# Weights packed by the host in the order of the chip's loads: a hybrid mixer block on one Trainium2 core

## The chip, the cores and the metric

The kernel runs on one core of one Trainium2 chip. The metric is device microseconds of one execution (lower is better). The kernel before takes 2065.49 us, the median of three runs (2064.67 to 2066.31). The host's work ahead of the launch, its packing of arrays included, is not in the time.

## The reference, cut to what matters

One block over 256 latent tokens and 256 context tokens of width D = 2048, all in float32. Six adaLN vectors come from a 2048 x 12288 matrix; the modulated tokens go through one wide projection, four groups of mixers (GLA, gated delta rule, a short convolution, RWKV-7), an output projection, and a SwiGLU of width 5632.

```python
def _modulation(cond, w, bias):
    m = jax.nn.silu(cond) @ w + bias
    return [a[:, None, :] for a in jnp.split(m, 6, axis=-1)]

m_x = _modulation(c, ada_w[l], ada_b[l])
m_c = _modulation(c_ctx[None, :], ada_w[l], ada_b[l])
o_c, ctx_states = _mix(_modnorm(h_c, norm1_g[l], m_c[0], m_c[1]), h_c.shape[1], zero, lp)
o_x, _ = _mix(_modnorm(h_x, norm1_g[l], m_x[0], m_x[1]), GRID_W, ctx_states, lp)   # n @ w_in ... y @ w_out
h_x = h_x + m_x[2] * o_x
h_x = h_x + m_x[5] * _swiglu(_modnorm(h_x, norm2_g[l], m_x[3], m_x[4]), ffn_w_gu[l], ffn_w_down[l])
return _rmsnorm(h_x, final_g)
```

Every weight is read from HBM: `ada_w` once (96 MB), `w_in` twice (context and latents), `w_out`, `w_gu` and `w_down` once.

## The kernel before, in words

P = 128 is a tile's width, KT = 16 the number of feature tiles, T = 256 the tokens of a sequence. Products are exact to float32: each weight tile `wraw` is split by ScalarE into an upper half `wh` (L156) and by VectorE into the rest `wl` (L161), and TensorE (PE) adds three products of halves. All loads of weights are issued by SyncE (SP) on one queue, in program order. The program has four stages.

**Start.** The context tokens (`xin`, two loads of 1 MB) are normed and turned. Then a loop over 16 feature tiles kt: `first_vectors(kt)` loads two 1 MB pieces of `ada_w` into `ad` (three buffers, L391), multiplies them with the two conditions (`ada`, 32 PE instructions), and makes the modulated tokens `nh`, `nl`; `early_weights(kt)` loads one row tile of 11 column tiles of `w_in` into `wr` (three buffers; seven loads, L415 and L419, 704 KB) and splits it; PE then adds 33 products into `acc`. PE takes the `ada` products of tile kt + 1 ahead of the `acc` products of tile kt.

**Mixers.** `proj` loads a column tile of `w_in` in four pieces of 256 KB into `wraw` (six buffers, L571) and adds its products into `big`; between them stand `ada_pieces`, steps of the later adaLN vectors: a 256 KB load (L255) and products into `ob`. The recurrences of the mixers (`la`, `lb`, `ea`, `eb`, `iv...`) run beside them. `spill` parks a projected tile in DRAM (`xr...<-xs`, L596), `fetch` loads it again (L602). The order of the pieces is written by hand in `ORDER`, with offsets in instructions; the order of single instructions is then settled by the tile scheduler from its own estimates of how long each step takes.

**Output projection** (`wout`, L1376, 256 KB loads) and **SwiGLU** (`w_gu` L1445 and `w_down` L1482, 512 KB loads into four wide buffers).

In each of these loads a partition of the chip reads rows of the reference's matrices, so that what lies together in HBM is 128 columns (512 bytes) in `ada_w`, `w_in` and `w_gu`, and 512 columns (2 KB) in `w_out`, `w_down` and two pieces of each `wr`.

Of the kernel before, what the change touches and what calls it, by code (L numbers as in the profile page):

```python
# [16 lines left out]
P = 128  # L17
D = 2048
# [26 lines left out]
LEVS = (16, 32, 64)  # L45

# [86 lines left out]

@with_exitstack
def block_kernel(ctx: ExitStack, tc: tile.TileContext, x, cx, ada_w, ada_b, w_in, w_out, w_gu, w_down,
                 final_g, consts, params, small, out):
# [105 lines left out]
    gate_dram = mk(dram, [2, D], "gated")  # L242

    def ada_pieces(ci, bank_of, tmp):
        """adaLN columns of one of the later vectors, in steps to be taken between other work"""
        st = {}

        def piece(j, kt):
# [3 lines left out]
            with tc.high_priority():  # L252
                raw = wraw()
                rv = raw.rearrange("p (g c) -> p g c", g=4)
                nc.sync.dma_start(rv, ada_w[kt * P:(kt + 1) * P, ci * D:(ci + 1) * D]  # L255
                                  .rearrange("p (g c) -> p g c", g=4)[:, :, j * P:(j + 1) * P])
# [37 lines left out]
    def open_bank(flat):  # L294
        """zeros in a PSUM bank, left open for sums in any order"""
# [21 lines left out]
    # block-diagonal tiles: off-diagonal blocks stay zero  # L317
# [21 lines left out]
    RUNS = [(n, NR) for n in ("r_k", "r_v")] + [(n, ND) for n in ("d_k", "d_v")]  # L339
    EARLY = [(n, i) for n, k in RUNS for i in range(k)]  # L340
# [4 lines left out]
    with ExitStack() as st:  # L345
# [37 lines left out]
        NE = len(EARLY) + 1  # L383
# [3 lines left out]
        def first_vectors(kt):  # L387
            """modulation of feature tile kt, and the modulated context tokens"""
            ad = mk(s0, [P, KT, 2, P], "ad", 3)
            for i in range(2):  # L390
                nc.sync.dma_start(ad[:, :, i, :], ada_w[:, i * D + kt * P:i * D + (kt + 1) * P]  # L391
                                  .rearrange("(k p) c -> p k c", p=P))
# [18 lines left out]
        def early_weights(kt):  # L411
            raw = mk(s0, [P, NE * P], "wr0", 3)
            rows = slice(kt * P, (kt + 1) * P)
            for (c0, w, c) in SMALLS:
                nc.sync.dma_start(raw[:, c:c + w], w_in[rows, c0:c0 + w])  # L415
            o = P
            for n, k in RUNS:
                if k:
                    nc.sync.dma_start(raw[:, o:o + k * P], w_in[rows, OFF[n]:OFF[n] + k * P])  # L419
                o += k * P  # L420
# [42 lines left out]
    def col_products(ps, wh, wl, a, first, last):  # L463
        """ps[:, 0] + ps[:, 1] += w @ a, w and a in exact halves"""
# [4 lines left out]
    def row_products(acc, aH, aL, wh, wl, first, last, j):  # L469
        """acc[j] += a @ w for one half of the tokens; a is stored transposed, both in exact halves"""  # L470
# [5 lines left out]
    # ================= mixers =================  # L476
    Y = mk(dram, [16, P, T], "Yd")
    with mix:
# [4 lines left out]
        def runsum(o, i, d, z):  # L483
            """running sums, forward or backward, starting anew where z is zero"""
# [12 lines left out]
        # recurrent states at the end of the context, parked  # L497
# [64 lines left out]
        def proj(nHL, segs):  # L562
            """w_in columns of segs, transposed: [columns, tokens] in PSUM"""
            H, L = nHL
            ps = PB([P, T], "big")
            for hf in range(4):
                with tc.high_priority():
                    raw = wraw()
                    rv = raw.rearrange("p (k c) -> p k c", k=4)
                    for (c0, w, o) in segs:  # L570
                        nc.sync.dma_start(rv[:, :, o:o + w],  # L571
                                          w_in[hf * 512:(hf + 1) * 512, c0:c0 + w].rearrange("(k p) c -> p k c", p=P))
# [12 lines left out]
        def pcol(nHL, name, i):  # L585
            return proj(nHL, [(OFF[name] + i * P, P, 0)])
# [4 lines left out]
        def spill(nHL, name, i, s=1):  # L591
            """project columns and park them"""
# [14 lines left out]
        def sigmoid(o):  # L607
            """o = sigmoid(o), o not under -87"""
# [4 lines left out]
        def silu_to(o, z, tag):  # L613
            """o = z * sigmoid(z)"""
# [14 lines left out]
            # diagonal blocks, one row per partition  # L629
# [5 lines left out]
            # rows r and 15 - r of a block hold 15 entries together; side by side, the second one backwards  # L635
# [8 lines left out]
            # all entries of a block on every partition of that block  # L644
# [72 lines left out]
        def smalls(sm):  # L717
            """gate inputs of low rank, and what hangs on them alone"""
            cur[0] = "b"
            # rows 0..15: inputs of the GLA gate; 32..39: running sums of the GDN log decay;  # L720
            # 64..127: shifted RWKV inputs
# [6 lines left out]
            for d in range(2):  # L728
# [7 lines left out]
                # tanh(z) = 2 sigmoid(2 z) - 1  # L736
# [6 lines left out]
            # Gated DeltaNet: log decay, its running sums, beta  # L743
# [4 lines left out]
            # softplus(z) = -logsig(-z)  # L748
# [22 lines left out]
            # sums over whole chunks, on every partition  # L771
# [5 lines left out]
            # rows 0..3 (forward) use the running sum, rows 4..7 (backward) the reversed one  # L777
# [19 lines left out]
        def rw_gates(p, d, sm):  # L797
            """sums of sigmoid(.) inside each chunk of 64 (the log decay over -RW_S), and a"""
# [21 lines left out]
        def halves(dst, src, eng):  # L820
            """src [P, 4, 64] -> the diagonal blocks of dst [P, 4, 2, 64]"""
# [18 lines left out]
        def rwkv(p, s, raw, sm):  # L840
# [6 lines left out]
            for d in range(2):  # L847
# [52 lines left out]
                # values, token-major  # L900
# [5 lines left out]
                # L and M  # L906
# [9 lines left out]
                # decayed keys, token-major  # L916
# [5 lines left out]
                # [nB | nA^T]  # L922
# [9 lines left out]
                # [K~ | A_rk^T], token-major  # L932
# [31 lines left out]
                for n, c in enumerate(order):  # L964
                    # [outputs | state]
# [37 lines left out]
        def conv(o, z, taps, s):  # L1003
            """three-tap convolution along rows of 256 (context) or 64 tokens"""
# [9 lines left out]
        def gdn(h, s, raw, sm):  # L1014
# [40 lines left out]
            # decays between tokens; index d * 2 + c  # L1055
# [95 lines left out]
        def gla(p, s, raw, sm):  # L1151
# [28 lines left out]
            for d in range(2):  # L1180
# [52 lines left out]
                for n, c in enumerate((0, 1, 2, 3) if d == 0 else (3, 2, 1, 0)):  # L1233
                    # [outputs | state]
# [85 lines left out]
        for tok in ORDER:  # L1320
            st, _, ofs = tok.partition(":")
            with tc.high_priority(offset=int(ofs)) if ofs else ExitStack():
# [8 lines left out]
                elif low == "xx":  # L1331
                    if c == 0:
                        nHL = load_nT()
                        smx = t1("rgate")
                        acopy(smx, proj(nHL, SMALLS))
# [36 lines left out]
        def wout(b, kts, acc):  # L1372
            for kt in kts:
                with tc.high_priority():
                    raw = wraw()
                    nc.sync.dma_start(raw, w_out[kt * P:(kt + 1) * P, b * 512:(b + 1) * 512])  # L1376
# [52 lines left out]
    # ================= SwiGLU =================  # L1429
# [5 lines left out]
    for f in range(FT):  # L1435
        # sums of the products with the tokens' upper parts, and with their lower ones
        pg = [mk(ps2, [P, 2, T], "acc", 8) for _ in range(2)]
        for k0, nk, bufs in ((0, 8, wide), (8, 4, narrow), (12, 4, narrow)) if f == 0 else ((0, 8, wide), (8, 8, wide)):
            w = []
            wp[:] = bufs  # L1440
            for u in range(2):
                c0 = u * FFN + f * P
                with tc.high_priority():
                    raw = wraw()
                    nc.sync.dma_start(raw.rearrange("p (k c) -> p k c", k=nk),  # L1445
                                      w_gu[k0 * P:(k0 + nk) * P, c0:c0 + P].rearrange("(k p) c -> p k c", p=P))
                    w.append(split(raw, V))
            # the first tile takes the tokens as they get ready
# [16 lines left out]
    # the table of the last norm's functions, ahead of it  # L1465
# [7 lines left out]
    for b in range(4):  # L1473
# [3 lines left out]
        for k2 in range(FT // 2):  # L1477
            # the last weights of all are kept for the halves of the tokens in turn
            tail = b == 3 and k2 >= FT // 2 - 4
            with tc.high_priority():  # L1480
                raw = wraw()
                nc.sync.dma_start(raw.rearrange("p (k c) -> p k c", k=2),  # L1482
                                  w_down[k2 * 256:(k2 + 1) * 256, sl].rearrange("(k p) c -> p k c", p=P))
# [27 lines left out]
def prepare(inputs):  # L1511
    """host side: arrays as the launch takes them"""
# [24 lines left out]
```

## Time and profile before

| what | value |
|---|---|
| time, median of 3 runs | 2065.49 us |
| span of the profiled execution | 2059.4 us |
| what lies around the span (median less span) | 6.1 us |
| start, up to 200 us | DMA engines busy 0.94 to 1.01 up to 184 us |
| mixers, output projection, 200 to 1320 us | PE busy 1070.1 of 1120 us |
| SwiGLU, 1333 to 2050 us | PE busy 716.6 of 717 us |

The span is from the first to the last instruction of one profiled execution; it is the profile's only time of it, so times below are from the span's start, and the 6.1 us around it are carried over. PE busy counts a matmul from its start to a modelled end, so that it overlaps with its neighbours. PEclk is the clock that was granted to TensorE, as a share of 2.4 GHz: 0.5 is 1.2 GHz. The DMA share is the mean busy share of the core's 16 DMA engines, and GB/s what they moved.

### The profile page before, as it was taken

What the parts mean: (1) busy time and instruction counts of PE and PEld (TensorE: products, weight loads), DVE (VectorE), ACT (ScalarE), POOL (GpSimd) and SP (SyncE); (2) the same over time, 40 slices, a digit from 0 to 9 for tenths busy, and PEclk for the clock granted to TensorE, in tenths of its full rate; (3) what the DMA queues carried; (4) which work ended last, traced back from release to release, by engine and by line L of the source; (5) the groups of instructions that cost most, each with busy time, mean ns of one, the idle gap of its engine ahead of it and who ended that gap; (6) DMA issues with size and microseconds to landing.
All of it is one profiled execution on the core that took longest, in us unless ns stands there. A gap on an engine that the chain in (4) does not pass through costs nothing.

```text
span 2059.4 us, 37523 instructions
## 1 busy us (share of the span) xinstructions
PE 1933.2 (94%) x13864; PEld 1640.5 (80%) x13864; DVE 1341.9 (65%) x3488; ACT 988.3 (48%) x2013; POOL 163.3 (8%) x210
## 2 busy tenths in 40 slices
PE   4777999979999999999999999899999999999998
PEld 2556787758887887888989978788888888888886
DVE  3333875788778957889897776655555555545554
ACT  2112644564456435555654565555555555544444
POOL 0000100000101000101010000200000000000000
PEclk9899999989999999999999999999999999999999
DMA  9997858834847748534333655466666666665554
GB/s 271 277 275 222 240 162 236 228 103 125 227 139 199 204 140 246 136 82 111 102 105 107 166 186 193 135 187 188 187 185 185 188 188 186 185 234 195 193 195 154
DMA packets 609272, 374.31 MB, mean 182 GB/s; under 512 B 31776, under 2 KB 570784, under 8 KB 608192
## 3 DMA queue, kind: packets, MB, share of 16 engines
q1 hardware_dynamic: 604176, 366.59, 61.3%
q10 hardware_dynamic: 4320, 3.15, 0.5%
q8 instruction: 109, 1.79, 0.4%
q0 software_dynamic: 592, 2.18, 0.3%
q14 instruction: 75, 0.61, 0.1%
HBM read 359.89 MB, written 11.94 MB: 181 GB/s over the span
## 4 chain that ended last, share of the span: by engine, by line
PE 73%; DMA 11%; DVE 8%; issue 3%; ACT 2%; POOL 1%; SPq 0%; ACTq 0%; DVEq 0%; POOLq 0%
PE acc L173 36%; PE big L173 14%; PE la L173 8%; DMA ad<-in_ada_w 6%; PE ea L173 4%; PE lb L173 4%; PE ob L173 3%; PE eb L173 3%; DVE wl L161 2%; DMA wraw<-in_w_in 2%; DMA wraw<-in_ada_w 1%; ACT wh L156 1%; DMA wr<-in_w_in 1%; DVE ivaXc L161 1%; DVE ivaw L161 1%
## 5 line engine op out<-in xcount | busy, mean ns | idle before, releaser
L161 DVE TENSOR_TENSOR wl<-wraw,wh 128x512 fp32r<-128x512 f32 x856 | 568.3, 690 | 417.8 <-ACT wh L156 410.0
L156 ACT ACTIVATE wh<-wraw 128x512 fp32r<-128x512 f32 x856 | 509.9, 625 | 544.6 <-PE acc L173 186.2
L173 PE MATMUL acc<-n,wh 128*128 128x512 f32 x1408 | 493.4, 399 | 3.0 <-ACT wh L156 3.0
L173 PE MATMUL acc<-n,wl 128*128 128x256 f32 x1408 | 382.7, 282 | 0.3 <-DVE wl L161 0.3
L173 PE MATMUL big<-nh,wh 128*128 128x256 f32 x1056 | 319.5, 303 | 0.9 <-ACT xs L156 0.9
L173 PE MATMUL big<-nl,wh 128*128 128x256 f32 x1056 | 308.2, 292 | 0.0
L173 PE MATMUL big<-nh,wl 128*128 128x256 f32 x1056 | 306.7, 291 | 1.2 <-DVE wl L161 1.2
L173 PEld LDWEIGHTS acc<-n,wh 128*128 128x128 f32 x1408 | 259.9, 189 | 59.9 <-ACT wh L156 3.3
L173 PEld LDWEIGHTS acc<-n,wl 128*128 128x128 f32 x1408 | 266.9, 190 | 9.3 <-DVE wl L161 0.8
L173 PEld LDWEIGHTS big<-nh,wh 128*128 128x128 f32 x1056 | 199.7, 189 | 29.6 <-issue 23.5
L173 PEld LDWEIGHTS big<-nh,wl 128*128 128x128 f32 x1056 | 199.9, 190 | 8.1 <-issue 5.2
L173 PEld LDWEIGHTS big<-nl,wh 128*128 128x128 f32 x1056 | 199.9, 189 | 7.3 <-issue 6.7
L173 PE MATMUL acc<-wl,hH 128*128 128x512 f32 x352 | 137.1, 389 | 0.0
L173 PE MATMUL acc<-wh,hH 128*128 128x512 f32 x352 | 137.0, 389 | 0.0
L173 PE MATMUL acc<-wh,hL 128*128 128x512 f32 x352 | 137.0, 389 | 0.0
L173 PE MATMUL ob<-wraw,sc 128*32 128x128 f32 x2048 | 110.4, 284 | 10.7 <-DMA wraw<-in_ada_w 7.0
L173 PEld LDWEIGHTS ob<-wraw,sc 128*32 128x32 f32 x2048 | 52.1, 109 | 45.4 <-DMA wraw<-in_ada_w 12.1
L173 PE MATMUL ada<-ad,sc 128*32 128x256 f32 x512 | 46.0, 510 | 37.6 <-DMA ad<-in_ada_w 35.5
L161 POOL TENSOR_TENSOR hL<-sg,hH 128x256 fp32r<-128x256 f32 x44 | 44.5, 1012 | 453.4 <-ACT hH L156 453.4
L173 PEld LDWEIGHTS acc<-wl,hH 128*128 128x128 f32 x352 | 66.1, 188 | 14.2 <-DVE wl L161 0.2
L173 PEld LDWEIGHTS acc<-wh,hH 128*128 128x128 f32 x352 | 66.1, 188 | 13.7
L173 PEld LDWEIGHTS acc<-wh,hL 128*128 128x128 f32 x352 | 66.1, 188 | 13.6
(473 smaller groups left out, 3130.6 us busy)
## 6 DMA issues: line engine op xcount, KB each, us to landing
wraw<-in_w_gu SPq DMA_DIRECT2D x174, 512.0 KB, 4.0
wraw<-in_w_in SPq DMA_DIRECT2D x260, 256.0 KB, 3.0
wraw<-in_ada_w SPq DMA_DIRECT2D x256, 256.0 KB, 3.7
wraw<-in_w_down SPq DMA_DIRECT2D x88, 512.0 KB, 4.3
ad<-in_ada_w SPq DMA_DIRECT2D x32, 1024.0 KB, 8.4
wraw<-in_w_out SPq DMA_DIRECT2D x64, 256.0 KB, 3.2
wr<-in_w_in SPq DMA_DIRECT2D x32, 256.0 KB, 4.0
xin<-in_cx SPq DMA_DIRECT2D x2, 1024.0 KB
```

Of the source, the lines that this page charges most:

```text
L156: A.activation(o, i, AF.Copy)
L161: (e or V).tensor_tensor(out=o, in0=a, in1=b, op=op)
L173: return TE.matmul(o, l, r, start=start, stop=stop)
```

## The change

The host lays each weight matrix out anew, so that one load reads for each partition one run: 2 KB for a piece of `w_in`, `w_out` and the later adaLN vectors, 4 KB for `w_gu` and `w_down`, 5632 bytes for a row tile of the early weights (a copy of their columns of its own, `w_early`), 8 KB for half of an `ad`. The same bytes land at the same places on chip. Three things change beside the runs: the seven loads of a `wr` are one, the three or more loads of a `SMALLS` piece in `proj` are one (12 loads become 4), and the two loads of an `ad` split it by the summed features, not by shift and scale. Comment lines are gone too, which moves line numbers.

```diff
@@ ada_pieces: piece
-                nc.sync.dma_start(rv, ada_w[kt * P:(kt + 1) * P, ci * D:(ci + 1) * D]
-                                  .rearrange("p (g c) -> p g c", g=4)[:, :, j * P:(j + 1) * P])
+                r0 = (((ci - 2) * 4 + j) * KT + kt) * P
+                nc.sync.dma_start(raw, ada_later[r0:r0 + P, :])
@@ first_vectors
             ad = mk(s0, [P, KT, 2, P], "ad", 3)
+            av = ada_first[kt * P:(kt + 1) * P, :].rearrange("p (k a c) -> p k a c", k=KT, a=2)
             for i in range(2):
-                nc.sync.dma_start(ad[:, :, i, :], ada_w[:, i * D + kt * P:i * D + (kt + 1) * P]
-                                  .rearrange("(k p) c -> p k c", p=P))
+                ks = slice(i * KT // 2, (i + 1) * KT // 2)
+                nc.sync.dma_start(ad[:, ks], av[:, ks])
@@ early_weights
             raw = mk(s0, [P, NE * P], "wr0", 3)
-            rows = slice(kt * P, (kt + 1) * P)
-            for (c0, w, c) in SMALLS:
-                nc.sync.dma_start(raw[:, c:c + w], w_in[rows, c0:c0 + w])
-            o = P
-            for n, k in RUNS:
-                if k:
-                    nc.sync.dma_start(raw[:, o:o + k * P], w_in[rows, OFF[n]:OFF[n] + k * P])
-                o += k * P
+            nc.sync.dma_start(raw, w_early[kt * P:(kt + 1) * P, :])
@@ proj
-                    rv = raw.rearrange("p (k c) -> p k c", k=4)
-                    for (c0, w, o) in segs:
-                        nc.sync.dma_start(rv[:, :, o:o + w],
-                                          w_in[hf * 512:(hf + 1) * 512, c0:c0 + w].rearrange("(k p) c -> p k c", p=P))
+                    nc.sync.dma_start(raw, w_in[r0:r0 + P, hf * 512:(hf + 1) * 512])
@@ wout
-                    nc.sync.dma_start(raw, w_out[kt * P:(kt + 1) * P, b * 512:(b + 1) * 512])
+                    nc.sync.dma_start(raw, w_out[(b * KT + kt) * P:(b * KT + kt + 1) * P, :])
@@ SwiGLU
-                    nc.sync.dma_start(raw.rearrange("p (k c) -> p k c", k=nk),
-                                      w_gu[k0 * P:(k0 + nk) * P, c0:c0 + P].rearrange("(k p) c -> p k c", p=P))
+                    nc.sync.dma_start(raw, w_gu[r0:r0 + P, k0 * P:(k0 + nk) * P])
...
-                nc.sync.dma_start(raw.rearrange("p (k c) -> p k c", k=2),
-                                  w_down[k2 * 256:(k2 + 1) * 256, sl].rearrange("(k p) c -> p k c", p=P))
+                r0 = (b * (FT // 2) + k2) * P
+                nc.sync.dma_start(raw, w_down[r0:r0 + P, :])
```

The scheduler settles the order anew with the changed loads. On SP, in the start's loop, this stood before for one feature tile (destination, source, shape, how often):

```order
L415 DMA wr_77_241<-in_w_in 128x32 x2
L415 DMA wr_77_241<-in_w_in 128x64
L419 DMA wr_77_241<-in_w_in 128x512 x2
L419 DMA wr_77_241<-in_w_in 128x128 x2
L391 DMA ad_253<-in_ada_w 128x16x128 x2
```

And this stands there now, for the first three feature tiles:

```order
L446 DMA wr_77_241<-in_w_early 128x1408
L425 DMA ad_247<-in_ada_first 128x2048 x2
L446 DMA wr_85_278<-in_w_early 128x1408
L425 DMA ad_284<-in_ada_first 128x2048 x2
L446 DMA wr_93_348<-in_w_early 128x1408
L425 DMA ad_354<-in_ada_first 128x2048 x2
```

The order of `wr` and `ad` is the same; nine issues of a feature tile have become three.

On PE, where the start's loop begins, the turns of the tokens (`pt<-ident,xin`, four to a pair of feature tiles) stood before ahead of the first `ada` products like this:

```order
L374 MATMUL pt_195<-ident_64,xin_161 128x128
L374 MATMUL pt_195<-ident_64,xin_169 128x128
...
L374 MATMUL pt_201<-ident_64,xin_161 128x128
L374 MATMUL pt_201<-ident_64,xin_169 128x128
...
L173 MATMUL ada_256<-ad_253,sc_82 32x256 x5
L374 MATMUL pt_207<-ident_64,xin_161 128x128
```

Now the first of them stands behind the first of eight turns:

```order
L407 MATMUL pt_177<-ident_64,xin_161 128x128
L407 MATMUL pt_177<-ident_64,xin_169 128x128
...
L208 MATMUL ada_250<-ad_247,sc_82 32x256
L407 MATMUL pt_183<-ident_64,xin_161 128x128
L407 MATMUL pt_183<-ident_64,xin_169 128x128
```

The first `ada` product has moved from behind the fifth turn to behind the first; eight products of the second `ada` now stand between the last turns too.

On SP, in the middle of the mixers, where the latents' first RWKV keys are parked (`xr_r_k<-xs`), this stood before; the weights of that tile's projection end with `wraw_8376`, 7 loads of `w_in` ahead of the store:

```order
L571 DMA wraw_8566<-in_w_in 128x4x128
L255 DMA wraw_8572<-in_ada_w 128x4x128
L255 DMA wraw_8578<-in_ada_w 128x4x128
L571 DMA wraw_8596<-in_w_in 128x4x128
L596 DMA xr_r_k_1853_8407<-xs_8284 128x256
L602 DMA gd_rk_7773<-xr_d_z_1503_6871 128x256
L255 DMA wraw_8602<-in_ada_w 128x4x128
```

And this stands there now, where that projection's weights end with `wraw_8272`, 5 loads of `w_in` ahead of the store:

```order
L596 DMA wraw_8397<-in_w_in 128x512
L291 DMA wraw_8403<-in_ada_later 128x512
L291 DMA wraw_8409<-in_ada_later 128x512
L596 DMA wraw_8432<-in_w_in 128x512
L291 DMA wraw_8438<-in_ada_later 128x512
L620 DMA xr_r_k_1853_8303<-xs_8180 128x256
L291 DMA wraw_8444<-in_ada_later 128x512
```

The store has moved forward by two loads of `w_in` and the pieces of `ada` between them; many parks and fetches of the mixers have moved by a few loads like this, forward or back.

## Rows read from the trace of the kernel before

**Rows 1.** The page: busy time of each engine, and the DMA engines' slices.
```profile
span 2059.4 us, 37523 instructions
PE 1933.2 (94%) x13864; PEld 1640.5 (80%) x13864; DVE 1341.9 (65%) x3488; ACT 988.3 (48%) x2013; POOL 163.3 (8%) x210
DMA  9997858834847748534333655466666666665554
```

**Rows 2.** Windows by stage: busy us (x instructions) by engine, PEclk, DMA share, GB/s.
```profile
39.00:184.00 145.00, 108.51 (x1003) 86.53 (x1007) 49.34 (x88) 25.62 (x30) 0.00 (x0) 0.89 1.01 276
184.00:200.00 16.00, 10.56 (x95) 8.42 (x96) 5.60 (x17) 3.40 (x9) 2.92 (x9) 0.89 0.28 103
200.00:1320.00 1120.00, 1070.08 (x8878) 914.82 (x8877) 873.97 (x2677) 582.98 (x1238) 101.83 (x141) 0.99 0.58 163
1333.00:2050.00 717.00, 716.60 (x3758) 612.30 (x3756) 391.90 (x660) 356.77 (x703) 53.67 (x50) 1.00 0.62 189
```

**Rows 3.** The chain that ended last, 39 to 184 us: shares, and two pieces.
```profile
by line: DMA ad<-in_ada_w 81.4%; DMA wr<-in_w_in 11.9%; PE ada L173 5.4%; SPq L391 2.4%; SPq L419 1.9%; issue 1.5%; SPq L415 1.0%; PE acc L173 0.5%; DVE n L167 0.3%; PE pt L173 0.2%; DVE modB L165 0.2%; DVE modA L167 0.1%
...
60.26 9.92 DMA ad<-in_ada_w
...
173.81 10.00 DMA ad<-in_ada_w
```

**Rows 4.** Timeline of the start: second and last `ada`, and what precedes the loop.
```profile
18.62 1.91 ACT L286 ACTIVATE junk<-xin 128x2048 f32<-128x2048 f32 x1 [3.43 <-DMA xin<-in_cx]
...
24.24 1.12 PE L374 MATMUL pt<-ident,xin 128*128 128x128 f32 x4 [0.78 <-DVE xnT L381]
...
26.14 1.12 PE L374 MATMUL pt<-ident,xin 128*128 128x128 f32 x4 [0.78 <-DVE xnT L381]
...
36.44 2.64 ACT L156 ACTIVATE wh<-wr 128x1408 fp32r<-128x1408 f32 x2 [15.26 <-PE pt L374]
38.35 1.63 DVE L161 TENSOR_TENSOR wl<-wr,wh 128x1408 fp32r<-128x1408 f32 x1
39.17 3.18 PE L173 MATMUL ada<-ad,sc 128*32 128x256 f32 x32 [1.26 <-DMA ad<-in_ada_w]
...
183.95 1.93 PE L173 MATMUL ada<-ad,sc 128*32 128x256 f32 x32
```

**Rows 5.** Timeline of one feature tile's work on PE, and the next wait.
```profile
100.88 1.93 PE L173 MATMUL ada<-ad,sc 128*32 128x256 f32 x32 [1.66 <-DMA ad<-in_ada_w]
...
107.10 0.28 PE L173 MATMUL acc<-nh,wl 128*128 128x256 f32 x1
...
111.72 3.42 PE L173 MATMUL ada<-ad,sc 128*32 128x256 f32 x32 [4.34 <-DMA ad<-in_ada_w]
```

**Rows 6.** Windows in which the DMA engines moved one kind of run.
```profile
15.00:16.00 1.00, 0.00 (x0) 0.00 (x0) 0.78 (x1) 0.19 (x1) 0.00 (x0) 1.00 0.99 408
183.00:186.00 3.00, 2.74 (x39) 1.72 (x38) 0.06 (x1) 0.00 (x0) 0.00 (x0) 1.00 0.97 395
1450.00:1550.00 100.00, 100.00 (x568) 86.92 (x567) 55.49 (x98) 51.44 (x105) 9.16 (x9) 1.00 0.64 186
1900.00:2000.00 100.00, 100.00 (x443) 82.81 (x442) 54.97 (x82) 45.13 (x82) 6.42 (x4) 1.00 0.58 195
```

**Rows 7.** DMA issues: out<-in, count, KB of each, median us to landing.
```profile
ad<-in_ada_w SPq DMA_DIRECT2D x32, 1024.0 KB, 8.4
...
consts<-in_consts SPq DMA_DIRECT2D x1, 898.0 KB
...
sw<-in_small SPq DMA_DIRECT2D x1, 768.0 KB
```

**Rows 8.** Line 571, loads of `w_in`: issues, who waited, us to landing.
```profile
L571 SPq DMA_DIRECT2D wraw<-in_w_in x272: 367/368/1222, 0.7 to 1182.1; - x136
...
  ACT wh L156: 83.9, 57
...
DMA to landing us min/median/max: 2.6/3.1/5.2
```

**Rows 9.** Line 1376, loads of `w_out` (2 KB runs): issues, us to landing.
```profile
L1376 SPq DMA_DIRECT2D wraw<-in_w_out x64: 327/328/664, 1183.5 to 1285.1; - x64
...
DMA to landing us min/median/max: 2.9/3.2/7.3
```

**Rows 10.** The chain through the mixers, 218 to 1320 us: shares, first and last weight load.
```profile
by line: PE big L173 25.8%; PE la L173 14.3%; PE ea L173 8.3%; PE lb L173 7.6%; PE ob L173 5.1%; PE eb L173 4.8%; DVE wl L161 4.4%; issue 3.9%; DMA wraw<-in_w_in 3.0%; DMA wraw<-in_ada_w 2.6%; ACT wh L156 2.3%; DVE ivaXc L161 1.1%; DVE ivaw
...
291.33 3.58 DMA wraw<-in_w_in
...
1139.24 2.88 DMA wraw<-in_w_in
```

**Rows 11.** A window of the mixers in which PE idled most.
```profile
400.00:450.00 50.00, 37.89 (x265) 27.68 (x263) 41.42 (x126) 26.20 (x62) 1.69 (x3) 0.86 0.47 131
```

More of the change, by code (lines that the diff above doesn't have):

```diff
@@ L45 @@
 LEVS = (16, 32, 64)
+TILES = ([("small", 0)] + [(n, i) for n, k in (
+    ("r_k", 4), ("r_v", 4), ("r_r", 4), ("d_k", 4), ("d_v", 4), ("d_q", 4), ("d_z", 4), ("g_k", 2), ("g_q", 2),
+    ("g_v", 4), ("g_r", 4), ("r_g", 1), ("c_c", 4), ("c_h", 4), ("c_b", 4)) for i in range(k)])
+TIDX = {t: i for i, t in enumerate(TILES)}
+RUNS = [(n, NR) for n in ("r_k", "r_v")] + [(n, ND) for n in ("d_k", "d_v")]
+EARLY = [(n, i) for n, k in RUNS for i in range(k)]
+NE = len(EARLY) + 1
 def _const_array():
@@ L131, in _pack_small, with _pack_w_in, cols, _pack_ada @@
     return out
+def _pack_w_in(w):
+    def cols(n, i):
+        if n == "small":
+            return np.concatenate([w[:, c0:c0 + k] for c0, k, _ in SMALLS], 1)
+        return w[:, OFF[n] + i * P:OFF[n] + (i + 1) * P]
+    tiles = np.stack([cols(*t).reshape(KT, P, P).transpose(1, 0, 2) for t in TILES])
+    early = np.concatenate([cols(*t).reshape(KT, P, P) for t in [("small", 0)] + EARLY], 2)
+    return np.ascontiguousarray(tiles.reshape(len(TILES) * P, KT * P)), np.ascontiguousarray(early.reshape(KT * P, -1))
+def _pack_ada(w):
+    a = w.reshape(KT, P, 6, KT, P)
+    first = a[:, :, 0:2].transpose(3, 1, 0, 2, 4).reshape(KT * P, KT * 2 * P)
+    later = w[:, 2 * D:].reshape(KT, P, 4, 4, 4, P).transpose(2, 4, 0, 1, 3, 5).reshape(4 * 4 * KT * P, 512)
+    return np.ascontiguousarray(first), np.ascontiguousarray(later)
+def _pack_ffn(w_gu, w_down, w_out):
+    gu = w_gu.reshape(KT, P, 2, FT, P).transpose(3, 2, 1, 0, 4).reshape(FT * 2 * P, KT * P)
+    down = w_down.reshape(FT // 2, 2, P, 4, 512).transpose(3, 0, 2, 1, 4).reshape(4 * (FT // 2) * P, 1024)
+    wo = w_out.reshape(KT, P, 4, 512).transpose(2, 0, 1, 3).reshape(4 * KT * P, 512)
+    return tuple(np.ascontiguousarray(t) for t in (gu, down, wo))
 @with_exitstack
-def block_kernel(ctx: ExitStack, tc: tile.TileContext, x, cx, ada_w, ada_b, w_in, w_out, w_gu, w_down,
-                 final_g, consts, params, small, out):
+def block_kernel(ctx: ExitStack, tc: tile.TileContext, x, cx, ada_first, ada_later, ada_b, w_in, w_early, w_out,
+                 w_gu, w_down, final_g, consts, params, small, out):
     nc = tc.nc
@@ L338, in block_kernel @@
     L0 = [mk(nT, [P, T], f"nl{kt}", 1, F32R) for kt in range(KT)]
-    RUNS = [(n, NR) for n in ("r_k", "r_v")] + [(n, ND) for n in ("d_k", "d_v")]
-    EARLY = [(n, i) for n, k in RUNS for i in range(k)]
     hand = ExitStack()
@@ L382, in block_kernel @@
         s2 = st.enter_context(tc.tile_pool(name="s2", bufs=1, reuse_waits="tile"))
-        NE = len(EARLY) + 1
         acc = [mk(ps0, [P, 2, T], f"acc{i}") for i in range((NE + 1) // 2)]
@@ L560, in block_kernel, with proj @@
         feed = []
-        def proj(nHL, segs):
+        def proj(nHL, which):
+            r0 = TIDX[which] * P
             H, L = nHL
@@ L585, in pcol @@
         def pcol(nHL, name, i):
-            return proj(nHL, [(OFF[name] + i * P, P, 0)])
+            return proj(nHL, (name, i))
         def t1(tag, bufs=1):
@@ L1334, in block_kernel @@
                         smx = t1("rgate")
-                        acopy(smx, proj(nHL, SMALLS))
+                        acopy(smx, proj(nHL, ("small", 0)))
                     else:
@@ L1441, in block_kernel @@
             for u in range(2):
-                c0 = u * FFN + f * P
+                r0 = (f * 2 + u) * P
                 with tc.high_priority():
                     raw = wraw()
-                    nc.sync.dma_start(raw.rearrange("p (k c) -> p k c", k=nk),
-                                      w_gu[k0 * P:(k0 + nk) * P, c0:c0 + P].rearrange("(k p) c -> p k c", p=P))
+                    nc.sync.dma_start(raw, w_gu[r0:r0 + P, k0 * P:(k0 + nk) * P])
                     w.append(split(raw, V))
@@ L1513, in prepare @@
     a = {k: np.ascontiguousarray(np.asarray(v)) for k, v in inputs.items()}
+    ada_first, ada_later = _pack_ada(a["ada_w"].reshape(D, 6 * D))
+    w_in, w_early = _pack_w_in(a["w_in"].reshape(D, -1))
+    w_gu, w_down, w_out = _pack_ffn(a["ffn_w_gu"].reshape(D, 2 * FFN), a["ffn_w_down"].reshape(FFN, D),
+                                    a["w_out"].reshape(D, D))
     arrays = {
-        "x": a["x"].reshape(T, D), "cx": a["ctx"].reshape(T, D), "ada_w": a["ada_w"].reshape(D, 6 * D),
-        "ada_b": a["ada_b"].reshape(1, 6 * D), "w_in": a["w_in"].reshape(D, -1),
-        "w_out": a["w_out"].reshape(D, D), "w_gu": a["ffn_w_gu"].reshape(D, 2 * FFN),
-        "w_down": a["ffn_w_down"].reshape(FFN, D), "final_g": a["final_g"].reshape(D),
+        "x": a["x"].reshape(T, D), "cx": a["ctx"].reshape(T, D), "ada_first": ada_first, "ada_later": ada_later,
+        "ada_b": a["ada_b"].reshape(1, 6 * D), "w_in": w_in, "w_early": w_early, "w_out": w_out, "w_gu": w_gu,
+        "w_down": w_down, "final_g": a["final_g"].reshape(D),
         "consts": CONSTS, "params": _pack_params(a), "small": _pack_small(a),
```

## The prediction

> **What bounds the kernel now.** I first read the page: PE is busy 94% of the span, and in the slices of the DMA engines the reader should see 9s at the left edge, 3 to 8 in the middle, and an even 5 to 6 at the right [rows 1]. One average hides stages with different limits, so I cut the span into windows [rows 2]. From 39 to 184 us the DMA engines are full (share 1.01, 276 GB/s) while PE is busy 108.5 of 145 us, at a mean granted clock of 0.89. From 200 to 1320 us PE is busy 1070.1 of 1120 us and the DMA share is 0.58. From 1333 to 2050 us PE is busy 716.6 of 717 us with a DMA share of 0.62. So DMA is the limit in the start alone. The chain that ended last says the same: from 39 to 184 us 81.4% of it is `ad` loads, which take about 10 us each because they queue, and 11.9% is `wr` loads [rows 3].
>
> The pace of the start is read from PE: the second `ada` starts at 39.17 and the last, the sixteenth, at 183.95 us [rows 4], 14 steps of 10.34 us. One step's work on PE goes from 100.88 to 107.38 us, 6.50 us at full clock; then PE waits 4.34 us for the next `ad` [rows 5]. One step's bytes are two `ad` loads of 1024 KB and 704 KB of `wr`, together 2752 KB or 2.818 MB; at 276 GB/s that is 10.21 us. So a step is DMA time plus 0.13 us.
>
> **The start: what longer runs are worth.** No window of before moves 8 KB weight runs, but there are near ones [rows 6]. From 183 to 186 us the constants come in, `consts` and `sw` of 898 and 768 KB over 128 partitions, that is 7 and 6 KB to a run [rows 7]: 395 GB/s at a share of 0.97. In 15 to 16 us, mostly 8 KB rows of `xin`, it is 408 GB/s at 0.99. With 2 KB runs (`w_down`, 1900 to 2000 us) 195 GB/s at 0.58 makes 336 GB/s of a full share; with 512-byte runs (`w_gu`, 1450 to 1550 us) 186 at 0.64 makes 291. The engines are equally full in the start, so the rate grows with the run. The changed start reads runs of 5.6 and 8 KB, and I take the row nearest to that, 395 GB/s: 7.13 us, and with the same 0.13 us a step of 7.26 us. That is still above PE's 6.50, so DMA stays the limit, barely.
>
> The loop doesn't begin earlier. The first `wl` ends at 39.98 us, after the turns of the tokens have let ScalarE go (its `wh` waited for `pt`) [rows 4]; only then is the first of three `wr` buffers free, and SP issues the fourth `wr`, with the fourth `ad` behind it. With 395 GB/s the first three tiles (8.45 MB, 21.4 us) are through by then: `xin` is done at 18.6 us [rows 4]. So the fourth `ad` lands at about 40 + 7.1 + 2 (an estimate of a load's fixed part: 2.6 us for the fastest 256 KB load [rows 8] less its 0.6 us at 395 GB/s) = 49.1 us, and the sixteenth 12 steps later, at 136.2 us. Now it lands just ahead of 183.95 us, at the end of its piece of the chain, 183.8 us [rows 3]. **Term 1: -47.6 us.**
>
> Bounds of this term. With the 2 KB rate, 336 GB/s, a step is 8.52 us, and the end 40 + 8.4 + 2 + 102.2 = 152.6: -31. With 408 GB/s, 6.9 us, for the fourth tile, and from then on PE's 6.50 us and the 0.13 us as the step, the end is 40 + 6.9 + 2 + 79.6 = 128.5: -55. Nothing is excluded between.
>
> The Trainium skill speaks against the change here. In "DMA: Bandwidth & Descriptors", section Specifications, it puts the smallest transfer for line rate at 512 B: by that the old runs are long enough and term 1 is zero. The trace disagrees, with 276 GB/s against 395 GB/s at equally full engines; no row here shows a run of 512 B that went faster.
>
> **The start, other edits.** `ad` is now split by summed features, so the first half of the products needs only the first of its two loads; before, every product needed both. Only the last step can gain, half of 1.93 us [rows 5]: **term 2: -1 us**. Six issues fewer for each tile free SP (each about 0.37 us, as in [rows 8]), but the queue of bytes is what is full, so nothing. The first `ada` products stand between earlier turns: one `wr` and half an `ad` (1.77 MB) come behind `xin` and take 4.5 us, so the first half is there at about 25 us with the fixed part; the second turn starts at 24.24 us and each takes 1.9 us [rows 4]. A delay of 1 us at most, within term 1's bounds. If that cover is gone, every us of it moves the fourth `wr` by as much.
>
> **The mixers.** Sixteen weight loads lie on the chain between 218 and 1320 us [rows 10], 5.6% of it or 61.7 us, 3.9 us each. The fastest load of `w_in` lands in 2.6 us, the median in 3.1 [rows 8]; so on the chain about 1.3 us each is queueing behind other loads. With 256 KB taking 0.90 us at 291 GB/s and 0.78 at 336, queueing shrinks by 13%: 16 x 1.3 x 0.13 = 2.7 us. Against that, `w_out`, which has had 2 KB runs all along, lands in 2.9 us at the fastest and 3.2 in the median [rows 9], no sooner than 512-byte loads; if every load on the chain got 0.3 us later it would cost 4.8 us. Between +2 and -10 (if all queueing halves), I take **term 3: -2 us**. The 83.9 us that ScalarE waits for `w_in` [rows 8] are mostly not PE's wait.
>
> The order of the mixers changes with the scheduler's estimates: parks and fetches move by a few loads on SP, as the store of `xr_r_k` does. The stage idles PE for 1120 - 1070.1 = 49.9 us [rows 2], so a new order could give or take some of it; one bad spot costs about what 400 to 450 us shows, 12.1 us of idle [rows 11]. Zero is my value, plus or minus 10 us.
>
> **Output projection and SwiGLU.** PE has no idle time to give back (0.4 us of 717), and loads are hidden behind its products. `w_out` keeps 2 KB runs. Nothing. If the cover went, a wait for one 512 KB load would show as an idle PE, and there is none now.
>
> **Sum.** The profiled execution's span is 2059.4 us; 2059.4 - 47.6 - 1 - 2 = 2008.8, and with the 6.1 us around it (2065.49 - 2059.4) **2015 us** against the median of 2065.49.
>
> **Rivals.**
>
> *The start gets slower than its DMA.* PE's 6.50 us hold at full clock, but the rows show groups of `ada` that take 3.42 us after a wait of 4.34 us instead of 1.93 [rows 5], and a mean granted clock of 0.89, so some of that stage ran at 1.2 GHz. If every step keeps such a dip, 6.50 + 1.49 + 0.4 of waiting makes 8.4 us and PE is the limit: 40 + 8.4 + 2 + 100.8 = 151.2, a gain of 33, 2030 us. Slow 8 KB runs, at the 2 KB rate, end there too. For it: both limits are close. Against: a step with 0.8 us of wait leaves little room for a dip.
>
> *The mixers gain more.* If most of the queueing on the chain and the idle spot at 400 us go too, another 20 us: 1995 us. For it: DMA is at 8 to 9 tenths in several slices of the mixers [rows 1]. Against: PE's long waits there are few.
>
> *512 bytes were long enough*, the rule above: the pace stays at 10.34 us and the time at 2065 us. Against it stand [rows 6].
>
> *Slower.* In the new order SP, which issues in program order, meets a store whose projection isn't done, and every weight load behind it waits, and PE with them. One such spot costs 12.1 us [rows 11]. It decides when five new spots appear: 60.5 us against 50.6, that is 2075 us. For it: the order was changed in many places and `ORDER`'s offsets belong to the old one. Against: parks have moved by a handful of loads, not by whole pieces, and six buffers lie ahead of them.
>
> **How the numbers follow.** Forecast with its bounds, 2000 to 2030 us: 65%. Slower start, 2030 to 2050: 18%. Mixers gain more, below 2000: 8%. No gain, within 0.2% (4.1 us, about what a measurement of this kernel can tell from no change): 5%. Slower: 4%. The range leaves out the upper part of the second case and nearly all of the last three: 2000 to 2037 us. Faster 0.91, same 0.05, slower 0.04.
>
> **What would show it.** In the profile after, `ada` should start every 7.1 to 7.5 us with the DMA share still near 1 and about 390 GB/s; the last `ada` near 136 us; the stage from there to the output projection as long as before to within 10 us; the SwiGLU window unchanged to 2 us. A DMA share clearly under 1 in the start with PE idle-free says the first rival; a distance from last `ada` to output projection that grew by tens of us says the last. The prediction is wrong if 8 KB runs of weights don't reach 395 GB/s or if the mixers' order costs more than 15 us.

## The result, and the profile after

The changed kernel takes 2037.27 us, the median of four runs (2033.7 to 2038.36), against 2065.9 us (2064.67 to 2067.62, four runs): a ratio of 0.985, with a 95% interval of 0.984 to 0.987. It is faster, by 28.6 us where 50.5 were forecast, and 0.3 us above the range.

Three rows of the page, to be read against [rows 1]: the span, PE, and the DMA engines in 40 slices.

```profile
span 2035.6 us, 37321 instructions
PE 1927.7 (95%) x13863; PEld 1635.8 (80%) x13864; DVE 1341.4 (66%) x3488; ACT 990.6 (49%) x2013; POOL 172.3 (8%) x210
DMA  8976478444565556333233466355555555576554
```

The nines of the DMA engines at the left edge have gone from three to one. The windows by stage, with columns as in [rows 2]; the second lies inside the first, where all engines are in the start's steady loop, and the third goes from the first product into `big` to the first product of the SwiGLU.

```profile
39.00:140.00 101.00, 89.38 (x907) 72.51 (x902) 45.18 (x83) 24.14 (x28) 1.45 (x1) 0.98 0.95 381
50.00:115.00 65.00, 58.59 (x605) 47.88 (x607) 28.12 (x54) 15.46 (x18) 0.00 (x0) 1.00 0.99 397
161.60:1281.70 1120.10, 1063.06 (x8833) 908.39 (x8829) 862.39 (x2652) 576.71 (x1222) 101.59 (x133) 0.99 0.52 162
1295.00:2020.00 725.00, 724.12 (x3796) 619.35 (x3797) 394.22 (x663) 360.54 (x707) 54.84 (x51) 1.00 0.58 189
```

The start moves 381 GB/s where it moved 276. The SwiGLU has 0.9 us of idle PE in 725; before it had 0.4 in 717 [rows 2]. The landmarks on PE come from the timeline: the first group of the last `ada`, the first `big`, and the first product of the SwiGLU (`acc<-n`).

```profile
144.72 1.07 PE L208 MATMUL ada<-ad,sc 128*32 128x256 f32 x16
161.64 0.58 PE L208 MATMUL big<-nh,wh 128*128 128x256 f32 x1
1281.68 0.78 PE L208 MATMUL acc<-n,wh 128*128 128x512 f32 x1
```

In the kernel before these stood at 183.95 [rows 4], 199.5 and 1306.0 us. So the first `big` came 37.9 us sooner, and the stretch from it to the SwiGLU grew from 1106.5 to 1120.0 us, by 13.5. That stretch (mixers and output projection) is called **the stretch** from here on.

The start shows no wait for `ad` any more. All that PE waits for between 48 and 140 us is this (us in total, times, longest; from 48 to 184 us the kernel before has 34.2 us of waits for `ad`):

```profile
PE pt L208 <- DVE row L432: 8.6, 12, 0.7
```

One step, from the timelines of ScalarE, VectorE, PE and SP (the number in brackets is the idle time before, with what ended it):

```profile
99.45 1.93 PE L208 MATMUL ada<-ad,sc 128*32 128x256 f32 x32
99.49 1.38 ACT L191 ACTIVATE wh<-wr 128x1408 fp32r<-128x1408 f32 x1 [2.04 <-PE acc L208]
100.90 1.63 DVE L196 TENSOR_TENSOR wl<-wr,wh 128x1408 fp32r<-128x1408 f32 x1 [3.00 <-ACT wh L191]
102.44 0.42 DVE L432 COPY row<-ada 128x256 f32<-128x256 f32 x1
102.92 0.61 PE L208 MATMUL pt<-csel,row 128*128 128x2 f32 x4 [0.73 <-DVE row L432]
...
106.84 0.42 PE L208 MATMUL ada<-ad,sc 128*32 128x256 f32 x4
```

When the products of one tile end, `wh` gets one of its two buffers back and ScalarE splits the tile after next. VectorE's `wl` follows, and the copy `row`, which takes 0.42 us and could have started when `ada` ended at about 101.4, stands behind it. PE, in its fixed order, reaches `pt` and waits 0.73 us. The step is 106.84 - 99.45 = 7.39 us, and no DMA lies on that loop.

### The profile page after: what moved, and what is told of

Read it like the earlier page. It is cut to its first block, busy times and chain, and to the rows that moved or that the text cites. A ratio compares the mean times of both kernels' runs of the same rounds, so it can differ in the third digit from the quotient of the medians.

```text
span 2035.6 us, 37321 instructions
## 1 busy us (share of the span) xinstructions
PE 1927.7 (95%) x13863; PEld 1635.8 (80%) x13864; DVE 1341.4 (66%) x3488; ACT 990.6 (49%) x2013; POOL 172.3 (8%) x210
## 4 chain that ended last, share of the span: by engine, by line
PE 74%; DVE 10%; DMA 8%; ACT 4%; issue 2%; POOL 1%; SPq 0%; ACTq 0%; DVEq 0%; POOLq 0%
PE acc L208 38%; PE big L208 13%; PE la L208 7%; PE ea L208 4%; DMA wraw<-in_w_in 4%; PE lb L208 4%; DVE wl L196 4%; ACT wh L191 3%; PE eb L208 3%; PE ob L208 2%; DMA ad<-in_ada_first 1%; DVE ivaw L196 1%; DVE ivaXc L196 0%; PE pt L208 0%; DMA wraw<-in_x 0%
## 5 line engine op out<-in xcount | busy, mean ns | idle before, releaser
L196 DVE TENSOR_TENSOR wl<-wr,wh 128x1408 fp32r<-128x1408 f32 x16 | 26.0, 1624 | 42.7 <-ACT wh L191 42.7
```

The source lines that it names most:

```text
L196: (e or V).tensor_tensor(out=o, in0=a, in1=b, op=op)
```

## The experiments

**One engine order for two layouts.** Does the new order cost the 13.5 us, or do the packed loads? These kernels fix the order in which each engine issues:

```python
for a, b in zip(seq, seq[1:]):   # seq: one engine's instructions in the order wanted
    tc.add_manual_dep(mine[b], mine[a].name, NoSync)
```

*packed_old_order:* 

> The packed kernel, with every instruction of the mixers and all that follows them put in the order of the kernel before on all five engines; the start keeps the packed kernel's own order. Between the first product into `big` and the first product of the SwiGLU the kernel before took 1106.5 us and the packed one 1120.0. Theory 'order' (the 13.5 us are the price of the new order): 1103 to 1110 us here, and a time of about 2024 us. Rival 'loads' (they are the price of the packed loads themselves, which land otherwise than before): 1117 to 1123 us, and about 2037 us. The start is as in the packed kernel under both: `ada` every 7.4 us.

*unpacked_new_order:* 

> The reverse: the kernel before with its old layout, its start in its old order, and from the mixers on the packed kernel's order on all five engines. Theory 'order': first `big` to first SwiGLU product takes 1117 to 1123 us, and the time is about 2079 us, slower than before by 13 us. Rival 'loads': 1104 to 1110 us, and about 2066 us. The start takes as long as before (`ada` every 10.3 us) under both.

**A third buffer.** The loop above is loosened by one more buffer for the upper halves:

```diff
-            wh = mk(s2, [P, NE * P], "wh0", 2, F32R)
+            wh = mk(s2, [P, NE * P], "wh0", 3, F32R)
```

*packed_wh3:* 

> The packed kernel with three buffers for the upper halves of the early weights (`wh0`) where it has two. Only the place of the split on ScalarE changes. Theory 'loop' (the start's 7.41 us step is a loop: the split of tile k+2 waits until the products of tile k let go of its buffer, VectorE's copy of the `ada` row stands behind that split, and PE waits 0.7 us for the row): the wait of PE for `row` goes, the step falls to 6.6 to 6.8 us (PE's 6.5 us or 2.82 MB at the 420 GB/s that the DMA engines reach when full), the last `ada` starts about 134 us and not 144.7, and the time is about 2027 us. Rival 'DMA' (the step is the DMA engines' own, 381 GB/s): the step stays at 7.3 to 7.5 us and the time at about 2037 us.

*packed_old_order_wh3:* 

> Both edits together: packed, old order from the mixers on, three `wh0` buffers. If both 'order' and 'loop' hold and their gains add, about 2037 - 13 - 10 = 2014 us; if 'order' alone, about 2024; if 'loop' alone, about 2027; if neither, 2037.

The times and stages, each from one profile (the pace is the mean of the eleven steps from the fourth `ada` to the fifteenth; PE idle is the stretch less PE's busy time in a window over it; before and after stand in the first and fifth row; the rows marked "again" and the two `ad_` rows belong to runs told further down):

| kernel | time us, median | pace of `ada` | first `big` | stretch | PE idle in it |
|---|---|---|---|---|---|
| before | 2065.9 | 10.32 | 199.5 | 1106.5 | 46.7 |
| before_again_1 | 2067.46 (one run) | 10.53 | 203.7 | 1106.8 | 45.7 |
| before_again_2 | 2068.69 (one run) | 10.57 | 204.6 | 1107.5 | 45.8 |
| unpacked_new_order | 2073.03 | 10.63 | 199.3 | 1121.4 | 58.3 |
| after | 2037.27 | 7.41 | 161.6 | 1120.0 | 57.0 |
| packed_again | 2038.6 (one run) | 7.41 | 161.2 | 1122.4 | 58.9 |
| ad_512_dense | 2052.95 (one run) | 8.73 | 178.5 | 1119.8 | 57.6 |
| ad_2k_dense | 2035.42 (one run) | 7.42 | 163.8 | 1116.7 | 55.5 |
| packed_xin_first | 2031.16 | 7.43 | 155.0 | 1119.0 | 55.0 |
| packed_wh3 | 2025.64 | 6.43 | 152.2 | 1118.8 | 54.5 |
| packed_old_order | 2022.9 | 7.43 | 154.9 | 1112.4 | 48.2 |
| packed_old_order_again | 2018.62 (one run) | 7.43 | 153.4 | 1110.8 | 48.8 |
| mixers_512_old_order | 2021.54 | 7.42 | 153.3 | 1113.3 | 49.7 |
| packed_old_order_wh3 | 2010.24 | 6.43 | 142.4 | 1116.6 | 53.5 |

The ratios to the kernel before, with 95% intervals: packed_old_order 0.978 [0.976, 0.980], unpacked_new_order 1.003 [1.001, 1.004], packed_wh3 0.980 [0.977, 0.982], packed_old_order_wh3 0.972 [0.969, 0.974].

*packed_wh3* did what theory "loop" says: the wait for `row` is gone, and in the same stretch of the start PE has no idle time left, with the DMA engines full:

```profile
50.00:115.00 65.00, 65.00 (x694) 54.40 (x694) 32.99 (x60) 17.96 (x20) 0.00 (x0) 0.99 1.01 419
```

In the loop PE and VectorE take a step's work in the same order as in the packed kernel. `row` now starts when `ada` ends, because `wl` no longer waits for `wh` (timeline of VectorE):

```profile
77.00 1.63 DVE L196 TENSOR_TENSOR wl<-wr,wh 128x1408 fp32r<-128x1408 f32 x1 [1.63 <-PE acc L208]
78.89 0.42 DVE L432 COPY row<-ada 128x256 f32<-128x256 f32 x1 [0.27 <-PE ada L208]
```

The step is 6.43 us, a little under the 6.6 to 6.8 expected; PE's work for a step had been read as 6.50. The rival "DMA" falls: the engines could do 419 GB/s. At that rate the 2.818 MB of a step take 6.73 us (worked out), so the pace of 6.43 also uses up tiles that were loaded ahead. The time is 11.6 us under that of the packed kernel.

*packed_old_order_wh3* takes 2010 us where 2014 was expected if the two gains add, but they don't add in the way that was meant. Against packed_wh3, 9.8 us lie ahead of the first `big`, for a reason that comes next, and only 2.2 us in the stretch (1118.8 to 1116.6), where theory "order" put some 13. With three buffers these profiles don't show the price of the order.

*packed_old_order* fits neither of its two ranges: 1112.4 us lies between. That its time, 2022.9 us, is near the 2024 of theory "order" is luck, since 6.7 us of the gain came from the start. Two things were mixed in it. Placing everything of the start ahead of everything of the mixers, which was meant to leave the start alone, also moved nine mixer loads of 256 KB. In the kernels before and after, SP issues some of them ahead of the context tokens (after, timeline of SP):

```profile
2.59 1.21 SPq L291 DMA_DIRECT2D wraw<-in_ada_later  x2
8.00 0.33 SPq L596 DMA_DIRECT2D wraw<-in_w_in  x1
8.37 0.43 SPq L397 DMA_DIRECT2D xin<-in_cx  x1
```

With the tokens first the first `big` comes 6.7 us sooner (154.9). *unpacked_new_order* has the stretch that theory "order" gave, 1121.4 us, but for the same reason a quicker start than a usual execution of the kernel before (199.3 against 204 us, below), and so 2073.03 and not 2079 us. The next two kernels keep the tokens first and vary one thing each.

*packed_xin_first:* 

> The packed kernel's own order on every engine, but everything of the start ahead of everything of the mixers: on SP nine 256 KB loads of mixer weights that stood ahead of the context tokens go behind the start, as they did in the packed kernel with the old order. That run gained 14.4 us, 6.7 of it before the first `big` (161.64 to 154.89 us) and 7.6 between the first `big` and the SwiGLU (1120.0 to 1112.4). This run holds the order of the mixers at the new one. If the new order costs 7.6 us: first `big` about 155 us, the stretch 1118 to 1122 us, the time about 2030.5 us. Rival (the order is worth nothing, the 7.6 us come with the nine loads or are chance): the stretch 1110 to 1114 us, the time about 2023 us.

*mixers_512_old_order* (the order of packed_old_order, instruction for instruction; `src` is a tile's 128 columns in the matrix that isn't packed, and the later adaLN loads are changed in the same way):

```diff
-                    nc.sync.dma_start(raw, w_in[r0:r0 + P, hf * 512:(hf + 1) * 512])
+                    nc.sync.dma_start(raw.rearrange("p (k c) -> p k c", k=4),
+                                      src[hf * 512:(hf + 1) * 512, :].rearrange("(k p) c -> p k c", p=P))
```

> The packed kernel with the old order from the mixers on and its start first (2022.9 us), instruction for instruction the same order, but the loads of `w_in` in `proj` and of the later adaLN vectors read runs of 512 bytes from matrices that are not packed. If 2 KB loads in the mixers are worth nothing either way: 2023 us to within 3, stretch from first `big` to SwiGLU 1110 to 1115 us. If 2 KB loads cost the mixers something (the stretch of the kernel before was 1106.5 us, 6 less): about 2017 us. If they help: above 2026 us.

Ratios: 0.984 [0.982, 0.986] and 0.978 [0.977, 0.980]. Both came out as the first reading of each has it. With the same start, the new order's stretch is 1119.0 us and the old one's 1112.4, a time of 2031.16 against 2022.9 us, 8.3 us (the profiled execution of packed_xin_first was the quickest of its five, that of packed_old_order the slowest of its four). With the old order, 512-byte loads give 1113.3 us and 2 KB loads 1112.4. The windows over the stretch, old order then new, show the difference as idle PE:

```profile
154.90:1267.30 1112.40, 1064.18 (x8832) 909.00 (x8829) 866.60 (x2661) 576.41 (x1226) 92.35 (x132) 0.98 0.53 164
```

```profile
155.00:1273.90 1118.90, 1063.90 (x8832) 908.66 (x8829) 865.22 (x2661) 578.35 (x1226) 100.15 (x132) 0.98 0.52 163
```

And the same for mixers_512_old_order and unpacked_new_order:

```profile
153.30:1266.60 1113.30, 1063.59 (x8832) 907.82 (x8829) 865.69 (x2661) 576.55 (x1226) 92.18 (x133) 0.98 0.58 164
```

```profile
199.30:1320.60 1121.30, 1063.00 (x8832) 906.85 (x8829) 866.13 (x2661) 577.68 (x1226) 99.81 (x132) 0.98 0.58 163
```

PE is busy for 1063 to 1064 us in all four; it idles 48.2 and 49.7 us under the old order, 55.0 and 58.3 under the new one. The table says the same of every kernel with two `wh0` buffers: 45.7 to 49.7 us with the old order and 55.0 to 58.9 with the new one, whichever layout is loaded.

The largest single part of it has a name. In the stretch PE waits 5.2 to 7.9 us for the latents' rows (`xs`, read from `in_x`) in all seven profiles with the new order, and 0.6 to 2.6 in all seven with the old one, third buffer or not. Over the stretch, packed_xin_first and then packed_old_order (us in total, times, longest):

```profile
PE big L577 <- DMA xs<-in_x: 5.2, 3, 3.2
```

```profile
PE big L577 <- DMA xs<-in_x: 1.8, 2, 1.3
```

Against that the old order has 4.0 to 4.6 us of waits at `ea` for `rw_BK`, and the new one 0.6 to 1.0. The rest is spread over waits that differ by 2 us or less each in the mean. No run changed one of these places alone.

Having the tokens first is worth less than it looks. Under the old order the same instructions can be set against each other one by one: from the first `big` of before_again_1 (203.7 us) to the product that it runs at 227 us, packed_old_order takes 6.1 us longer, and keeps most of that to the end (5.4 us at the product that stands at 1268 us). The mixers begin without the weights that were loaded early, and what the start gained is given back there. That accounts for 1112.4 against 1106.8 us in the old order; it is read from the two timelines, and no run tested it by itself.

**Run length or scatter.** The old loads differ from the new in two ways: short runs, and rows spread over a whole matrix. Two kernels keep each 1 MB load of `ad` one dense block and only cut its runs. This is the host's side of the first, cut; the loads follow with the same shape:

```diff
-        first = a[:, :, 0:2].transpose(3, 1, 0, 2, 4).reshape(KT * P, KT * 2 * P)
+        first = a[:, :, 0:2].transpose(3, 0, 2, 1, 4).reshape(KT * KT * 2 * P, P)
```

*ad_512_dense:* 

> The packed kernel, but each 1 MB load of `ad`, still one dense block of HBM, reads it in runs of 512 bytes (the wr loads keep 5.6 KB). Read from the start alone. Theory 'run length' (what a partition reads in one run sets the rate): `ad` at about 276 GB/s takes 7.6 us a step and `wr` 1.7 us at 420 GB/s, a step of 9.0 to 9.6 us with a DMA share near 1. Rival 'dense' (it is the scatter of the old rows over HBM that cost): the step stays at 7.3 to 7.6 us.

*ad_2k_dense:* 

> The same with runs of 2 KB. Theory 'run length': by the 336 GB/s of 2 KB runs in the SwiGLU of the kernel before, 6.24 + 1.7 = 7.9 us a step, DMA share near 1. Rival 'dense': 7.3 to 7.6 us.

The window 50 to 115 us, first with 512-byte runs, then with 2 KB:

```profile
50.00:115.00 65.00, 55.23 (x537) 44.10 (x526) 25.84 (x48) 13.69 (x16) 0.00 (x0) 0.92 1.02 306
```

```profile
50.00:115.00 65.00, 58.60 (x611) 47.41 (x604) 28.88 (x54) 15.98 (x18) 0.00 (x0) 1.00 1.04 393
```

With 512-byte runs the first steps live on what was loaded ahead, and from 78.67 us on the mean of nine steps is 9.25 us, in the range of "run length"; the kernel took 2052.95 us in one run. So dense blocks alone don't help much: the run counts. (A quarter of the bytes, `wr`, came in 5.6 KB runs in both; in the kernel before they had runs of 2 KB and less.) With 2 KB the expectation of 7.9 us failed: 393 GB/s, the step stays at 7.43 us (the loop's), 2035.42 us. That is no evidence for "dense", since the 512-byte run rules it out; the 336 GB/s taken for 2 KB runs was too low for this stage. How fast 2 KB runs are where the loop doesn't hold them was not run.

**Chance.** One profile of each kernel might mislead, so the two kernels and the old order were profiled once more (rows in the table).

*before_again_1:* 

> The kernel before, unchanged, profiled once more. Its one profile so far has a span of 2059.4 us, and 1106.5 us from the first `big` to the first product of the SwiGLU. If that execution was a quick one (its median time of 2065.5 to 2067 us, less about 2 us around the span, is a span of 2063.5 to 2065), the span is 2062 to 2068 us, with the excess in that stretch: 1109 to 1114 us. Rival (the stretch repeats and the packed kernel loses all of 13.5 us there): 1105 to 1108 us in that stretch, whatever the span.

*before_again_2:* 

> The same once more, with the same two readings: 1109 to 1114 us if the first profile was of a quick execution, 1105 to 1108 us if the stretch repeats.

*packed_again:* 

> The packed kernel, unchanged, profiled once more: its stretch from the first `big` to the SwiGLU was 1120.0 us, and 1119.0 us with the same order in the run with the tokens first. It should repeat to within 2 us, since its times spread less than those of the kernel before; if it comes out under 1116 us, chance accounts for more of the loss than the order.

*packed_old_order_again:* 

> The packed kernel with the old order from the mixers on, profiled once more: the stretch was 1112.4 us. If the order's price is 7 to 8 us, 1110 to 1114 us here again; above 1117 us, the two orders can't be told apart.

The first profile of before was of a quick execution, as supposed, but the place was wrong: the stretch repeats within 1 us (1106.8, 1107.5), and most of the excess (4.2 and 5.1 of 6.0 and 7.2 us) is in the start, where the pace was 10.53 and 10.57 us and not 10.32. The window of before_again_1, against the first of [rows 2], shows fewer bytes at equally full engines (268 GB/s, not 276):

```profile
39.00:184.00 145.00, 113.35 (x966) 88.90 (x967) 47.52 (x87) 24.23 (x29) 0.00 (x0) 0.82 0.99 268
```

Of the packed kernel, the stretch repeats within 2.4 us, where 2 were expected, and the old order's came out at 1110.8, as it should if the order has a price. The two `ad_` kernels run the packed kernel's mixers in its order, with 1119.8 and 1116.7 us, so a single stretch is good to some 3 us either way. With the means of the two later profiles of before and the two of after the sum closes: first `big` 204.1 to 161.4 us, -42.7; stretch 1107.2 to 1121.2 us, +14.0; together -28.7, with 28.6 timed (what follows the stretch adds another -1.1).

## Why the prediction was right in direction and short in size

28.6 us came where 50.5 were forecast, so 21.9 are missing. By the sum above, 5.9 of them are the start's (-42.7 us for the -48.6 of terms 1 and 2) and 16.0 the mixers' (+14.0 us for the -2 of term 3 and the zero for the order).

**What bounds the start, and that longer runs lift it: right.** At full shares the rate went from 276 GB/s [rows 2] to 397 between 50 and 115 us and, where nothing else held the loads, 419. The Trainium skill gives 512 B as the smallest transfer for line rate ("DMA: Bandwidth & Descriptors", Specifications). The runs of this stage disagree: 306 GB/s with 512-byte `ad` runs in dense blocks, 393 with 2 KB. That no row showed a faster run of 512 B passes over the prediction's own 291 GB/s for `w_gu`; next to 395 it changes nothing.

**Term 1 failed in "DMA stays the limit, barely" and in the step of 7.26 us.** The rate of 395 GB/s was not too high; the engines simply weren't the limit any more. Their share didn't tell: it is 0.99 in the packed kernel's loop, which they don't limit, and 1.01 with the third buffer. What told of the limit in the kernel before was PE's wait for `ad`. PE's 6.50 us for a step were set beside the DMA time as if PE could run them back to back. The wait for `row` behind `wl` was not seen, because in the kernel before it lay under the 4.34 us that PE waited for `ad` [rows 5]. The step became 7.41 us. That this lies within the 7.1 to 7.5 us named as a sign is luck: another loop set it. The second miss is the catching up. The loop did begin at the forecast's place (the fourth `wr` is issued at 40.22 us, for 40). The fourth `ad` was forecast to land at 49.1 us and its products to follow at once. But PE began the `acc` products at 41 us, with all sixteen tiles' still to do and those of two ahead of the fourth `ada`; this window lies in the first of them:

```profile
44.00:48.00 4.00, 4.00 (x27) 3.84 (x30) 0.98 (x3) 0.56 (x2) 0.00 (x0) 0.67 1.01 418
```

PE was busy throughout, part of it at 1.2 GHz (a mean granted clock of 0.67), and the fourth `ada` started at 54.97, 5.9 us late. The twelve steps from there are 7.48 us in the mean and not 7.26, the last of them 8.21, which is another 2.6 us: the last `ada` stands at 144.72 and not 136.2 us. With the third buffer it starts at 135.28 us: the forecast's place, reached by an edit that the change did not have. **Term 2** did not show as a gain: the last `ada` is now issued in two halves with `acc` products between, and from its start to the first `big` 16.9 us pass, where it was 15.6.

**Term 3, -2 us, failed in its sign.** The value "zero, plus or minus 10" for the order was the mis-sized part. With the tokens first the order costs 6.6 to 8.2 us (1119.0 against 1112.4 and 1110.8). The sign named for this, the stage as long as before to within 10 us, was missed. The loads themselves changed the mixers by less than the runs can tell (1113.3 against the same two). Between before and after, which both keep the early loads, the stretch differs by 14.0 us, and only order and layout differ; so the rest is put down to the order as well. Instruction by instruction, counted from the first `big` of each, the packed kernel is 6.2 us ahead of packed_xin_first at 185 us and has lost that lead by 755 us. The direct pair, packed with the old order and the early loads kept, was not run, so of the 14 us some 7 are shown and the others argued. The mechanism of the rival *slower* was not what happened: no wait of 12 us appeared. The idle PE is spread over many short waits, none over 4.3 us in the kernels with the new order; the largest difference is the wait for the latents' rows above, with single waits up to 3.3 us.

**SwiGLU: right**, 743.2 us from first to last product before and 744.2 after. **The 6.1 us around the span** were two things: about 2 us that lie around every execution (2037.38 - 2035.6 = 1.8; 2067.46 - 2065.4 = 2.1), and 4 us by which the profiled execution was quicker than the median, most of it in its start. The sum comes out the same, but a row of that start was a little too good to stand for the median.

**The rivals.** *The start gets slower than its DMA* came nearest: PE's own chain became the limit. Its mechanism, a clock dip in each step, was wrong; the granted clock is 1.00 in the steady loop. The time falls into its band, 2030 to 2050 us, but mostly through the mixers.

**What stays open.** packed_old_order_wh3 has a stretch of 1116.6 us, 3 to 6 us more than the other packed kernels with this order, and 53.5 us of idle PE. Its mixers begin 12 us sooner, and instruction by instruction it loses 3.0 us between 605 and 805 us of packed_old_order's time. Its profile is of the slowest of four executions (2013.81 us; the quickest took 2006.81), so part of this may be chance; why was not settled. It is still the best version here: 2010.24 us, a ratio of 0.972, packed, with the old order and a third `wh0` buffer. Which of the places where the order changed costs the time was not separated by a run either.

## What to carry to other kernels

Where a load runs at full DMA engines, lengthen its runs: 512 bytes to 2 KB was most of it here. Before claiming the whole gap to the next limit, follow the loop that is left once that wait is gone, buffer by buffer and through the queue of each engine: a wait of 0.7 us that hid under one of 4.3 becomes the limit. A share near 1 doesn't say by itself that the engines set the pace. And where a scheduler's estimates set the order, a change of layout is also a change of order: pin the order and time the two apart.

## What the runs showed of the hardware that was not expected

One core took in 418 to 419 GB/s from HBM over 65 us with 5.6 and 8 KB runs, more than the constants' 395 [rows 6]. The pace of full engines on 512-byte rows varies from execution to execution (10.32, 10.53, 10.57 us a step). The packed loop's repeats to 0.02 us, but the DMA engines don't set it, so it isn't shown that longer runs make them steadier.
